# Seven block products for layer 1's up projection, and x kept in DRAM, in a two-layer trunk on one Trainium2 core

## The chip, the core and the metric

The kernel runs on one core of one Trainium2 chip. Its engines are TensorE (PE, with its weight loads as PEld), VectorE (DVE), ScalarE (ACT), GpSimd (POOL) and SyncE (SP), each with an instruction queue of its own that runs in order. The metric is the device time of one execution in microseconds (us). The frame in which the kernel is written (Tile) has a scheduler: the order of each engine's instructions follows from the program, its priorities and its tile pools, and is fixed before the run.

## What is computed

One step of a two-layer trunk on 640 tokens (512 sample tokens, 128 prompt tokens) with model width 1024. Layer 0 has a mixer of attention and gated MLP, layer 1 a bidirectional mLSTM; both end in the same FFN. The part that the change touches:

```python
def _modulate(x, w, shift, scale):
    return _rmsnorm(x, w) * (1 + scale) + shift

def _conv_ffn(h, w_up, cw, cb, w_down):
    a, g = jnp.split(h @ w_up, 2, axis=-1)
    return (jax.nn.gelu(_dwconv3(a, cw, cb)) * g) @ w_down

        h = _modulate(x, norm2_w[l], sh2, sc2)
        x = x + g2 * _conv_ffn(h, w_up[l], fconv_w[l], fconv_b[l], w_down[l])
    y_sample = _rmsnorm(x, final_norm_w)
```

`_dwconv3` is a three-point convolution along the tokens. All data are float32; the hidden width is 22 × 128.

## The kernel before

Activations lie with features on the 128 partitions and the 640 tokens along the free axis, as 8 tiles `x[k]` of 128 features (k-tiles) with two token halves of 320 (`HF`). A float32 product is made from three matmuls in the fp32r type: each operand is split in a high part (a cast, on ACT) and a low part (the difference, on DVE), and `proj` adds high·high, high·low and low·high. A product of 1024 features to 128 outputs for both halves is 8 × 3 × 2 = 48 matmuls of 320 columns.

Weights come through `wload`: one DMA on SP's queue into a tile `wraw`, the cast into `whi` (L181), the low part into `wlo` (L183), each in a ring of three tiles of 1024 columns in the pool `wp`, open for the whole kernel.

The FFN (`ffn`, for both layers the same code) runs over the 22 blocks f of the hidden width. Each block has two up products, a (s = 0) and g (s = 1). `conv3` copies a from PSUM to `fca` (L310, ACT), scales it (L313, ACT) and adds the two neighbours with four DVE instructions, for the 512 and the 128 tokens apart (L317, L319: 511 and 127 columns). Then come the gelu (L336, ACT), the product with g from PSUM (L337, DVE) and the split into high and low (L197 ACT, L198 DVE).

`GROUPS` cuts the 22 hidden tiles into three groups of 8, 7 and 7. After the first block of the following group come the 8 down products of the group before (`down`): each loads its weights, makes its product over the group's hidden tiles, and adds it into x[o] in SBUF with `residual` (L273: 320, 192 and 128 columns, as the token halves and the two segments cut them). The last group goes through `out_halves`: first the 8 outputs of token half 0, then the 8 of half 1, with sums of squares on ACT (L214) and POOL or DVE (L215); the steps of half 0's statistics and final norm (L224 to L240, L997) are run among half 1's products.

`start_three` starts the FFN: the first three up products, whose second token half is worked k-tile by k-tile as the norm of that half (`norm_k`: L247 DVE, L252 and L254 ACT, L256 DVE or POOL) delivers its tiles. In layer 1 `between` is empty.

The PSUM tiles come from `mm` (tags A with two buffers, B with one; each tile is two banks) and `misc` (two buffers of one bank).

Of the kernel before, what the change touches and what calls it, by code (L numbers as in the profile page):

```python
# [16 lines left out]
P = 128  # L17
# [9 lines left out]
GROUPS = ((0, 8), (8, 15), (15, 22))  # L27
# [18 lines left out]
def trunk(ctx: ExitStack, tc: tile.TileContext, I, O):  # L46
# [4 lines left out]
    wp = ctx.enter_context(tc.tile_pool(name="wp", bufs=3))  # L51
# [3 lines left out]
    misc = ctx.enter_context(tc.tile_pool(name="misc", bufs=2, space=PSUM))  # L55
    modx = ExitStack()
# [187 lines left out]
    def norm_k(pool, xk, rb, l, js, jc, k, hl, a0, a1):  # L244
# [3 lines left out]
        hf = pool.tile([P, w], F32, tag="hf", name=nm("hf"), bufs=2)  # L248
# [74 lines left out]
    def ffn(pool, x, hs, l, acc, between, done, late):  # L323
        def up(f, s):
            for _ in range(1 + (f %3 == 1)):
                if between:
                    between.pop(0)()
            hi, lo = wload(I["w_up"][l, f, s], KT * P)
# [13 lines left out]
        def down(g, hid):  # L342
            f0, f1 = GROUPS[g]
            for o in range(KT):
                if between:
# [776 lines left out]
```

## Time and profile before

| | |
|---|---|
| time, median of 3 runs (lowest to highest) | 1606.4 us (1603.39 to 1609.57) |
| the profiled execution's own time | 1606.81 us |
| its span, first to last instruction | 1605.0 us |
| mean granted clock of TensorE | 0.992 |
| layer 1's FFN in the chain | one piece of matmuls from 1146.90 us, 425.52 us long |

The page's first part gives the busy time of each engine as a share of the span. [...] The chain of waits follows the work that ended last back from step to step. A row of the table by line and form gives the busy time, the mean of one instruction in ns, and the idle time of the engine just ahead of these instructions with what ended it.

### The profile page before, as it was taken

Reading aid. Unit: us, or ns where it says so; the run is one execution under the profiler, and the core shown is the slowest. Engines: PE = TensorE matmul, PEld = TensorE weight load, DVE = VectorE, ACT = ScalarE, POOL = GpSimd, SP = SyncE. Lnnn points to the kernel's source line nnn. Section 1 sums busy time; section 2 is a strip of 40 time slices with the busy share of each in tenths; the row PEclk is TensorE's granted clock in tenths of the full one; section 3 lists DMA queues with packets and bytes.
Section 4 is the critical chain, followed back from the end, with each engine's and each line's share of the span. In section 5 each row is a group of like instructions: output and inputs, shape, how many; then the busy total and the mean of one; then the engine's idle time right before and its main releaser. Section 6 shows DMA issues by size and latency. Waiting matters only on the chain.

```text
span 1605.0 us, 26031 instructions
## 1 busy us (share of the span) xinstructions
PE 1561.2 (97%) x10560; PEld 1501.9 (94%) x10560; DVE 960.0 (60%) x1738; ACT 712.7 (44%) x1171; POOL 120.1 (7%) x116
## 2 busy tenths in 40 slices
PE   5999999999999999999989999999999999999997
PEld 4888889999999999999988999999999999999996
DVE  5547776769894889444775575667544334433445
ACT  5646665563312331334587564635633223312342
POOL 1100002300000000002300000013100000000012
PEclk9999999999999999999998999999999999999998
DMA  9424444436562555224523213234322222222233
GB/s 359 149 73 146 150 146 172 134 101 201 170 208 89 176 176 175 83 62 123 165 69 95 85 57 90 66 135 128 93 79 79 67 79 79 65 81 79 72 107 112
DMA packets 60167, 191.60 MB, mean 119 GB/s; under 512 B 6764, under 2 KB 10348, under 8 KB 59920
## 3 DMA queue, kind: packets, MB, share of 16 engines
q1 hardware_dynamic: 60048, 189.95, 37.2%
q8 instruction: 83, 1.36, 0.4%
q14 instruction: 36, 0.29, 0.1%
HBM read 181.95 MB, written 7.97 MB: 118 GB/s over the span
## 4 chain that ended last, share of the span: by engine, by line
PE 86%; DVE 6%; ACT 4%; issue 2%; DMA 2%; POOL 0%; SPq 0%; POOLq 0%; DVEq 0%; ACTq 0%
PE mm L193 72%; PE mm L827 2%; PE mm L805 2%; DVE wlo L183 1%; PE mm L401 1%; PE mm L403 1%; PE mm L802 1%; PE mm L402 1%; DMA mw<-w_mod 1%; PE misc L562 1%; ACT whi L181 1%; DVE xr L247 1%; ACT hf L252 1%; PE misc L109 1%; PE mm L532 1%
## 5 line engine op out<-in xcount | busy, mean ns | idle before, releaser
L193 PE MATMUL mm<-h,whi 128*128 128x320 f32 x3744 | 726.7, 312 | 3.4 <-ACT rows L612 1.6
L193 PEld LDWEIGHTS mm<-h,whi 128*128 128x128 f32 x3744 | 595.4, 189 | 9.7 <-ACT fca L310 1.9
L181 ACT CAST whi<-wraw 128x1024 fp32r<-128x1024 f32 (+2 forms) x229 | 233.0, 1019 | 586.6 <-PE mm L193 551.5
L193 PE MATMUL mm<-h,wlo 128*128 128x320 f32 x1872 | 444.8, 311 | 3.4 <-DVE wlo L183 3.4
L183 DVE TENSOR_TENSOR wlo<-wraw,whi 128x1024 fp32r<-128x1024 f32 (+2 forms) x229 | 272.7, 1191 | 232.8 <-ACT whi L181 226.3
L193 PE MATMUL mm<-hid,whi 128*128 128x320 f32 x1920 | 393.1, 310 | 1.8 <-ACT hid L197 0.7
L193 PEld LDWEIGHTS mm<-h,wlo 128*128 128x128 f32 x1872 | 318.9, 189 | 5.3 <-DVE wlo L183 4.2
L193 PEld LDWEIGHTS mm<-hid,whi 128*128 128x128 f32 x1920 | 310.4, 188 | 4.7 <-ACT hid L197 1.4
L193 PE MATMUL mm<-hid,wlo 128*128 128x320 f32 x960 | 255.5, 309 | 0.2 <-DVE wlo L183 0.2
L193 PEld LDWEIGHTS mm<-hid,wlo 128*128 128x128 f32 x960 | 169.7, 188 | 0.4 <-DVE wlo L183 0.4
L273 DVE SCALAR_TENSOR_TENSOR x<-mm,mod,x 128x192 f32<-128x192 f32 (+2 forms) x192 | 75.3, 433 | 139.9 <-PE mm L193 135.6
L136 DVE SCALAR_TENSOR_TENSOR mj<-mw,crow 128x1024 f32<-128x1024 f32 x112 | 136.6, 1219 | 1.0
L215 POOL TENSOR_TENSOR acc<-acc,sq 128x320 f32<-128x320 f32 x48 | 61.7, 1284 | 910.0 <-ACT sq L214 880.1
L337 DVE TENSOR_TENSOR fct<-fct,mm 128x640 f32<-128x640 f32 x44 | 36.1, 820 | 97.5 <-PE mm L193 94.1
L336 ACT ACTIVATE fct<-fct 128x640 f32<-128x640 f32 x44 | 32.3, 738 | 84.5 <-DVE fct L319 84.5
L252 ACT ACTIVATE hf<-xr,mod 128x192 f32<-128x192 f32 (+2 forms) x88 | 47.5, 575 | 22.6 <-DVE mod L174 8.8
L247 DVE TENSOR_TENSOR xr<-x,rb 128x320 f32<-128x320 f32 (+1 forms) x56 | 38.0, 694 | 24.9 <-ACT hf L252 13.7
L317 DVE SCALAR_TENSOR_TENSOR fct<-fca,vec,fct 128x511 f32<-128x511 f32 x88 | 44.9, 547 | 11.9 <-ACT fct L313 11.9
L319 DVE SCALAR_TENSOR_TENSOR fct<-fca,vec,fct 128x511 f32<-128x511 f32 x88 | 44.7, 544 | 0.0
L313 ACT ACTIVATE fct<-fca,vec 128x640 f32<-128x640 f32 x44 | 40.5, 925 | 1.3
L214 ACT ACTIVATE sq<-x 128x320 f32<-128x320 f32 x70 | 32.2, 468 | 16.7 <-DVE x L273 15.0
L541 ACT ACTIVATE p<-mm,mx 128x640 f32<-128x640 f32 (+1 forms) x40 | 28.4, 711 | 17.8 <-DVE mx L540 17.6
(249 smaller groups left out, 1491.6 us busy)
## 6 DMA issues: line engine op xcount, KB each, us to landing
wraw<-w_up SPq DMA_DIRECT2D x88, 512.0 KB, 3.7
mw<-w_modT SPq DMA_DIRECT2D x56, 512.0 KB, 4.3
wraw<-w_down SPq DMA_DIRECT2D x48, 448.0 KB, 3.3
mw<-w_mod SPq DMA_DIRECT2D x40, 512.0 KB, 5.9
wraw<-w_out SPq DMA_DIRECT2D x32, 512.0 KB, 3.6
wraw<-w_down SPq DMA_DIRECT2D x16, 512.0 KB, 3.6
x<-xT SPq DMA_DIRECT2D x16, 320.0 KB, 5.5
wraw<-w_qk SPq DMA_DIRECT2D x8, 512.0 KB, 3.5
```

The source lines that it names most:

```text
L136: V.scalar_tensor_tensor(out=junk, in0=w, scalar=1.0, in1=crow[:, r], op0=ALU.mult, op1=ALU.mult, accum_out=mod[:, l, j, k, r:r + 1])
L181: S.copy(hi[:, :n], raw[:, :n])
L183: V.tensor_tensor(out=lo[:, :n], in0=raw[:, :n], in1=hi[:, :n], op=ALU.subtract)
L193: T.matmul(ps[:, b, :HF], w, hs[k][:, part, b * HF:b * HF + HF], start=(k == 0 and i == 0), stop=(k == n - 1 and i == 2))
L215: (eng or V).tensor_tensor(out=acc[:, sl], in0=acc[:, sl], in1=sq, op=ALU.add)
L247: V.tensor_tensor(out=xr, in0=xk[:, a0:a1], in1=rb, op=ALU.mult)
L252: S.activation(out=hf[:, a:b], in_=xr[:, a:b], func=AF.Identity, scale=mod[:, l, jc, k, r:r + 1], bias=mod[:, l, js, k, r:r + 1])
L273: V.scalar_tensor_tensor(out=xo[:, a:b], in0=pa, scalar=mod[:, l, j, o, r:r + 1], in1=xo[:, a:b], op0=ALU.mult, op1=ALU.add)
L313: S.activation(out=t, in_=a, func=AF.Identity, scale=w1, bias=b)
L317: V.scalar_tensor_tensor(out=t[:, s + 1:e], in0=a[:, s:e - 1], scalar=w0, in1=t[:, s + 1:e], op0=ALU.mult, op1=ALU.add)
L319: V.scalar_tensor_tensor(out=t[:, s:e - 1], in0=a[:, s + 1:e], scalar=w2, in1=t[:, s:e - 1], op0=ALU.mult, op1=ALU.add)
L337: mark[0] = V.tensor_tensor(out=h2(t), in0=h2(t), in1=pg[:, :, :HF], op=ALU.mult)
```

## The change

Layer 0 keeps its code path. In layer 1's FFN:

- Blocks 0 to 2 (`PLAIN` = 3) are computed as before. Blocks 3 to 21 get their two up products for both token halves by a form of Strassen's scheme: the product is seen as 2 × 2 blocks (two halves of the 1024 features against a and g, two token halves) and formed by seven block products in place of eight. `prod` is one of them: 4 k-tiles × 3 = 12 matmuls of 320 columns. `fold_first` makes the first, `fold_main` five more, `fold_last` the last; it runs after the next block's `fold_first` in the program.
- The combinations of activations are made once: `fold_step`, four times, during blocks 1 and 2, on DVE, with a split on ACT and DVE. For that, `norm_k` keeps the norm's float32 result (f0, f1).
- The combinations of weights are made per block in `weights`: four DMAs of 256 KB, four adds on DVE, casts of 3 × 1024 and 512 on ACT, low parts of the same widths on DVE. Its rings are of their own (`zr`, `zw`, `rd`, `zd`); block 3 takes the old ring's tiles, which is then closed and opened again for the down weights with 640 columns.
- The partial results are gathered in two banks of one PSUM tile (b1, b4) and one of `misc` (b2), with ACT copies (L440, L441, L445, L447) and DVE adds (L449, L452, L455).
- The down products go in five groups of 5, 5, 4, 4 and 4 hidden tiles; two to four of them are issued per block. They no longer add into x in SBUF: `enter` stores x to DRAM (`xd2`), each down product loads its x[o] and stores it again on POOL's queue, and the memory of x serves the new rings. For the last group x is loaded back on SP's queue.

```diff
-GROUPS = ((0, 8), (8, 15), (15, 22))
+GROUPS = (((0, 8), (8, 15), (15, 22)), ((0, 5), (5, 10), (10, 14), (14, 18), (18, 22)))
+PLAIN = 3
...
-    wp = ctx.enter_context(tc.tile_pool(name="wp", bufs=3))
...
+    wx = ctx.enter_context(ExitStack())
+    ring = [wx.enter_context(tc.tile_pool(name="wp", bufs=3, side="right")), 1024]
...
     def wload(src, n, key="w"):
-        raw = wp.tile([P, 1024], F32, tag="wraw", name=nm("wraw"), bufs=3)
+        wp, width = ring
+        raw = wp.tile([P, width], F32, tag="wraw", name=nm("wraw"), bufs=3)
         nc.sync.dma_start(out=raw[:, :n], in_=src)
-        hi = wp.tile([P, 1024], F32R, tag="whi", name=nm("whi"), bufs=3)
+        hi = wp.tile([P, width], F32R, tag="whi", name=nm("whi"), bufs=3)
         S.copy(hi[:, :n], raw[:, :n])
-        lo = wp.tile([P, 1024], F32R, tag="wlo", name=nm("wlo"), bufs=3)
+        lo = wp.tile([P, width], F32R, tag="wlo", name=nm("wlo"), bufs=3)
         V.tensor_tensor(out=lo[:, :n], in0=raw[:, :n], in1=hi[:, :n], op=ALU.subtract)
-        return hi, lo
+        return hi, lo, raw
...
+        def down(g, hid, o, tag=None):
+            f0, f1 = groups[g]
+            if between:
+                between.pop(0)()
+            hi, lo, _ = wload(I[f"w_down{l}_{g}"][o], (f1 - f0) * P)
+            ps = mm_tile(tag)
+            if xd is not None:
+                xo = zq[0].tile([P, NT], F32, tag="xs", name=nm("xs"), bufs=3)
+                nc.gpsimd.dma_start(out=xo, in_=xd[o])
+            else:
+                xo = x[o]
+            proj(ps, hi, lo, hid)
+            residual(xo, ps, l, 5, o, 0, NT)
+            if xd is not None:
+                nc.gpsimd.dma_start(out=xd[o], in_=xo)
+
+        def prod(out, w, i, rhs, start):
+            for j in range(4):
+                c = slice(i * 512 + j * P, i * 512 + j * P + P)
+                for n, (h, part) in enumerate(((0, 0), (0, 1), (1, 0))):
+                    T.matmul(out, w[h][:, c], rhs(j, part), start=(start and j == 0 and n == 0),
+                             stop=(j == 3 and n == 2), skip_group_check=not start)
+
+        def split(w, src, n):
+            S.copy(w[0][:, :n], src[:, :n])
+            V.tensor_tensor(out=w[1][:, :n], in0=src[:, :n], in1=w[0][:, :n], op=ALU.subtract)
+            return w
+
+        def weights(f):
+            def pair(pool_, tag, n, bufs):
+                return [pool_.tile([P, n], F32R, tag=tag + p, name=nm(tag), bufs=bufs) for p in ("hi", "lo")]
+
+            def raw():
+                if f == PLAIN:
+                    return ring[0].tile([P, 1024], F32, tag="wraw", name=nm("wraw"), bufs=3)
+                return zp[0].tile([P, 1024], F32, tag="zr", name=nm("zr"), bufs=3)
+
+            def parts():
+                return pair(ring[0], "w", 1024, 3) if f == PLAIN else pair(zp[0], "zw", 1024, 5)
+
+            ra, rb, rc = raw(), raw(), raw()
+            if f == PLAIN:
+                rd, wd = zp[0].tile([P, 1024], F32, tag="zr", name=nm("zr"), bufs=3), pair(zp[0], "zw", 1024, 5)
+            else:
+                rd, wd = zq[0].tile([P, 512], F32, tag="rd", name=nm("rd"), bufs=1), pair(zq[0], "zd", 512, 1)
+            src = I["w_up"][l, f]
+            lo_, hi_ = slice(0, 512), slice(512, 1024)
+            nc.sync.dma_start(out=rd[:, lo_], in_=src[1][:, hi_])
+            nc.sync.dma_start(out=ra[:, lo_], in_=src[0][:, lo_])
+            nc.sync.dma_start(out=rc[:, hi_], in_=src[1][:, lo_])
+            nc.sync.dma_start(out=rb[:, lo_], in_=src[0][:, hi_])
+            V.tensor_tensor(out=ra[:, hi_], in0=rc[:, hi_], in1=rd[:, lo_], op=ALU.add)
+            wa = split(parts(), ra, 1024)
+            V.tensor_tensor(out=rb[:, hi_], in0=ra[:, hi_], in1=ra[:, lo_], op=ALU.add)
+            wb = split(parts(), rb, 1024)
+            V.tensor_tensor(out=rc[:, hi_], in0=rc[:, hi_], in1=ra[:, lo_], op=ALU.add)
+            V.tensor_tensor(out=rc[:, lo_], in0=rb[:, lo_], in1=rb[:, hi_], op=ALU.add)
+            wc = split(parts(), rc, 1024)
+            wd = split(wd, rd, 512)
+            return wa, wb, wc, wd
+        def fold_first(f, w):
+            px = mm_tile("A")
+            b1 = px[:, 0, :HF]
+            prod(b1, w[0], 0, lambda j, p: part_of(hs[j], p, 0), True)
+            return px
+
+        def fold_main(f, w, px):
+            b1, b4, b2 = px[:, 0, :HF], px[:, 1, :HF], aux[f % 2][:, :HF]
+            seed = f > PLAIN + 1
+            a = pool.tile([P, NT], F32, tag="fca", name=nm("fca"), bufs=1)
+            g = pool.tile([P, HF], F32, tag="fcg", name=nm("fcg"), bufs=2)
+            lo_, hi_ = slice(0, HF), slice(HF, NT)
+            prod(b4, w[0], 1, lambda j, p: fold[j](0, p), True)
+            with tc.high_priority(200):
+                S.copy(b2 if seed else a[:, lo_], b1)
+                S.copy(g, b4)
+            prod(b2, w[1], 0, lambda j, p: part_of(hs[j + 4], p, 0), not seed)
+            prod(b1, w[1], 1, lambda j, p: fold[j](1, p), False)
+            with tc.high_priority(200):
+                S.copy(a[:, hi_], b1)
+                if seed:
+                    S.copy(a[:, lo_], b2)
+                else:
+                    V.tensor_tensor(out=a[:, lo_], in0=b2, in1=a[:, lo_], op=ALU.add)
+            prod(b4, w[2], 0, lambda j, p: part_of(hs[j + 4], p, 1), False)
+            with tc.high_priority(200):
+                V.tensor_tensor(out=a[:, hi_], in0=b4, in1=a[:, hi_], op=ALU.add)
+            prod(b1, w[2], 1, lambda j, p: fold[j](2, p), False)
+            with tc.high_priority(200):
+                V.tensor_tensor(out=g, in0=b1, in1=g, op=ALU.add)
+            return conv(f, None, a), g
+
+        def fold_last(f, w, px, t, g):
+            b1 = px[:, 0, :HF]
+            prod(b1, w[3], 0, lambda j, p: fold[j](3, p), False)
+            for sl, q in ((slice(0, HF), b1), (slice(HF, NT), g)):
+                V.scalar_tensor_tensor(out=t[:, sl], in0=t[:, sl], scalar=-1.0, in1=q, op0=ALU.mult, op1=ALU.mult)
+            return store(f, t)
...
+        hids = [hidden(f) for f in range(PLAIN)]
+        enter()
+        zp[0] = zc.enter_context(tc.tile_pool(name="zp", bufs=1))
+        aux = [ms_tile() for _ in range(2)]
+        group_of = {f: g for g, (f0, f1) in enumerate(groups) for f in range(f0, f1)}
+        w = weights(PLAIN)
+        open_, todo = None, []
+        for f in range(PLAIN, NF):
+            g = group_of[f]
+            px = fold_first(f, w)
+            if open_ is not None:
+                hids.append(fold_last(*open_))
+            if f > PLAIN and group_of[f - 1] != g:
+                f0, f1 = groups[g - 1]
+                todo = [(g - 1, hids[f0:f1], o) for o in range(KT)]
+            if f == PLAIN:
+                t, gg = fold_main(f, w, px)
+                wx.close()
+                ring[:] = [wx.enter_context(tc.tile_pool(name="wq", bufs=3, side="right")), 640]
+                zq[0] = zc.enter_context(tc.tile_pool(name="zq", bufs=1))
+                nxt = weights(f + 1)
+                open_, w = (f, w, px, t, gg), nxt
+                continue
+            nxt = weights(f + 1) if f + 1 < NF else None
+            t, gg = fold_main(f, w, px)
+            n = min(len(todo), 4 if g and groups[g - 1][1] - groups[g - 1][0] == 5 else 3)
+            for i in range(n):
+                down(*todo.pop(0), "AB"[(n - i) % 2])
+            open_ = (f, w, px, t, gg)
+            w = nxt
+        hids.append(fold_last(*open_))
+        zc.close()
+        return hids[groups[-1][0]:]
...
+        def fold_step(j):
+            if j == 0:
+                tt.extend([hl_tile(hidp, "hid") for _ in range(2)])
+            d = hidp.tile([P, 4, HF], F32, tag="hid", name=nm("fd"), bufs=9)
+            b11, b12, b21, b22 = f0[j], f1[0][:, j], f0[j + 4], f1[1][:, j]
+            V.tensor_tensor(out=d[:, 0], in0=b11, in1=b12, op=ALU.subtract)
+            V.tensor_tensor(out=d[:, 2], in0=b22, in1=b12, op=ALU.subtract)
+            V.scalar_tensor_tensor(out=d[:, 1], in0=d[:, 0], scalar=-1.0, in1=b22, op0=ALU.mult, op1=ALU.subtract)
+            V.scalar_tensor_tensor(out=d[:, 3], in0=d[:, 1], scalar=-1.0, in1=b21, op0=ALU.mult, op1=ALU.subtract)
+            for i in range(2):
+                hilo(tt[2 * j + i], d[:, 2 * i:2 * i + 2].rearrange("p i c -> p (i c)"))
...
+        xd2 = dram.tile([KT, P, NT], F32, name="xd2")
+
+        def enter():
+            for k in range(KT):
+                nc.gpsimd.dma_start(out=xd2[k], in_=x[k])
+            sc.close()
+
+        hid = ffn(xp, x, hs, 1, [lambda j=j: fold_step(j) for j in range(4)], late, fold, enter, xd2)
+        ep = c0.enter_context(tc.tile_pool(name="ep", bufs=1))
+        acc = ep.tile([P, NT], F32, name=nm("acc"), tag="acc")
+        x = [ep.tile([P, NT], F32, name=nm("x"), tag=f"x{k}") for k in range(KT)]
...
+        for step in out_halves(ep, x, lambda o: I["w_down1_4"][o], 4, 1, 5, hid, acc, xd2, done1):
```

`part_of` in `proj` lets an operand be a function of part and half, `hidden` and `conv` are the former `hidden` in two pieces, and the host cuts `w_down` by the new groups.

What the scheduler makes of it on DVE, at the entry, where block 3's weights are first made. Before, this is the end of the convolution of block 1 and the beginning of that of block 2 (`wlo` are the low parts of up weights, `fct` the convolution, `hid` the hidden tile):

```order
L337 TENSOR_TENSOR fct_11662<-fct_11662,mm_11611 128x640 [waits PE_49,Activation_49]
L198 TENSOR_TENSOR hid_11602<-fct_11594,hid_11602 128x640 [waits Activation_49]
L183 TENSOR_TENSOR wlo_11800<-wraw_11796,whi_11798 128x1024 [waits DMAHW5_49]
L198 TENSOR_TENSOR hid_11670<-fct_11662,hid_11670 128x640 [waits Activation_49]
L183 TENSOR_TENSOR wlo_11855<-wraw_11851,whi_11853 128x1024 [waits DMAHW6_49,PE_49,Activation_49]
L317 SCALAR_TENSOR_TENSOR fct_11785<-fca_11783,vec,fct_11785 128x511 [waits Activation_49]
L317 SCALAR_TENSOR_TENSOR fct_11785<-fca_11783,vec,fct_11785 128x127
L319 SCALAR_TENSOR_TENSOR fct_11785<-fca_11783,vec,fct_11785 128x511 [waits DVE_49]
```

Now (`fd` are the folded activations and the tile written beside them their low part; `zr` and `wraw` block 3's raw weights, `w` their high and low parts):

```order
L204 TENSOR_TENSOR h_11368<-fd_11699,h_11368 128x640 [waits Activation_49]
L1177 SCALAR_TENSOR_TENSOR fd_11763<-fd_11763,f_1728_10727 128x320 [waits DVE_49]
L204 TENSOR_TENSOR hid_11611<-fd_11763,hid_11611 128x640 [waits Activation_49]
L326 SCALAR_TENSOR_TENSOR fct_11829<-fca_11827,vec,fct_11829 128x511
L204 TENSOR_TENSOR hid_11612<-fd_11763,hid_11612 128x640 [waits Activation_49]
L328 SCALAR_TENSOR_TENSOR fct_11829<-fca_11827,vec,fct_11829 128x511 [waits DVE_49]
L326 SCALAR_TENSOR_TENSOR fct_11829<-fca_11827,vec,fct_11829 128x127
L416 TENSOR_TENSOR wraw_11854<-wraw_11856,zr_11857 128x512 [waits DMASW4_49,DMASW5_49,DMASW3_49,DMASW6_49,DMASW2_49,DMASW7_49,DMASW1_49,DMAHW0_49,DMASW0_49,DMAHW6_49,PE_49,Pool_49]
L328 SCALAR_TENSOR_TENSOR fct_11829<-fca_11827,vec,fct_11829 128x127 [waits DVE_49]
L418 TENSOR_TENSOR wraw_11855<-wraw_11854 128x512 [waits DMAHW5_49,DVE_49]
L420 TENSOR_TENSOR wraw_11856<-wraw_11856,wraw_11854 128x512
L390 TENSOR_TENSOR w_11866<-wraw_11854,w_11865 128x1024 [waits Activation_49]
```

The first add of block 3's weights (L416) now stands behind the fold steps and most of block 2's convolution, and the first low part (L390) behind two more adds.

On PE, in the middle of the stage, where the b2 product of block 9 begins (`mm_13014` holds b1 and b4, `misc` b2, `mm_13329` a down product, `zw` the weights; `tt`, `h` and `hid` on L385 the activations):

```order
L385 MATMUL mm_13014<-h_11367,zw_12922 128x320 x2
L385 MATMUL mm_13014<-h_11367,zw_12923 128x320
L385 MATMUL mm_13014<-hid_11611,zw_12922 128x320 x2
L385 MATMUL mm_13014<-hid_11611,zw_12923 128x320
L199 MATMUL mm_13329<-hid_12908,wlo_13327 128x320
L385 MATMUL misc_11853<-h_11269,zw_12927 128x320 [waits Activation_49]
L385 MATMUL misc_11853<-h_11269,zw_12927 128x320
L385 MATMUL misc_11853<-h_11269,zw_12928 128x320
L385 MATMUL misc_11853<-h_11275,zw_12927 128x320 x2
L385 MATMUL misc_11853<-h_11275,zw_12928 128x320
L385 MATMUL misc_11853<-h_11317,zw_12927 128x320 x2
L385 MATMUL misc_11853<-h_11317,zw_12928 128x320
```

Before, products of 48 or 42 followed each other here with no wait for a copy within one; now one matmul of another product stands between the end of b4 and the product that waits for ACT's copy.

On SP's queue, at the change of rings after block 3:

```order
L414 DMA wraw_11856<-w_up 128x512 [waits DMAHW3_49,DVE_49]
L415 DMA wraw_11855<-w_up 128x512 [waits DMAHW4_49,DVE_49]
L412 DMA zr_11857<-w_up 128x512 [waits DMASW3_49,DMASW2_49,DMASW4_49,DMASW1_49,DMASW5_49,DMASW0_49,DMASW6_49,DVE_49,DMASW7_49,PE_49,Pool_49]
L413 DMA zr_11977<-w_up 128x512
L414 DMA zr_11979<-w_up 128x512
L415 DMA zr_11978<-w_up 128x512 [waits DMAHW0_49,DVE_49,Activation_49]
L412 DMA rd_11980<-w_up 128x512 [waits DMAHW6_49,DMAHW5_49,DMAHW7_49,DVE_49,PE_49]
L182 DMA wraw_12271<-w_down_0 128x640
L182 DMA wraw_12314<-w_down_0 128x640
L182 DMA wraw_12357<-w_down_0 128x640
```

Block 4's second g weight (`rd`) waits for PE, and the first loads of down weights stand behind it.

## Rows read from the trace of the kernel before

**Rows 1.** The page, part 1: busy us, share of the span, instructions of each engine.

```profile
PE 1561.2 (97%) x10560; PEld 1501.9 (94%) x10560; DVE 960.0 (60%) x1738; ACT 712.7 (44%) x1171; POOL 120.1 (7%) x116
```

**Rows 2.** Windows of 100 us: PE, PEld, DVE, ACT, POOL busy, PEclk, DMA share, GB/s.

```profile
400.00:500.00 100.00, 100.00 (x684) 100.00 (x683) 79.22 (x133) 25.15 (x28) 0.00 (x0) 1.00 0.57 178
...
1300.00:1400.00 100.00, 100.00 (x684) 100.00 (x683) 39.52 (x56) 32.52 (x38) 0.00 (x0) 1.00 0.24 73
```

**Rows 3.** Chain of waits, from 1130 us: start us, us, what.

```profile
1146.90 425.52 PE mm L193 x2898
```

**Rows 4.** DVE by line and form, 1100 to 1605 us: busy us, mean ns, idle before.

```profile
L183 DVE TENSOR_TENSOR wlo<-wraw,whi 128x1024 fp32r<-128x1024 f32 x56 | 68.8, 1228 | 95.5 <-ACT whi L181 95.5
...
L337 DVE TENSOR_TENSOR fct<-fct,mm 128x640 f32<-128x640 f32 x22 | 18.1, 821 | 56.7 <-PE mm L193 56.7
L317 DVE SCALAR_TENSOR_TENSOR fct<-fca,vec,fct 128x511 f32<-128x511 f32 x22 | 16.5, 751 | 7.6 <-ACT fct L313 7.6
...
L273 DVE SCALAR_TENSOR_TENSOR x<-mm,mod,x 128x320 f32<-128x320 f32 x24 | 13.2, 550 | 77.8 <-PE mm L193 77.8
L273 DVE SCALAR_TENSOR_TENSOR x<-mm,mod,x 128x192 f32<-128x192 f32 x30 | 12.3, 410 | 8.7 <-PE mm L193 8.6
...
L247 DVE TENSOR_TENSOR xr<-x,rb 128x320 f32<-128x320 f32 x16 | 10.3, 658 | 5.5 <-ACT rb L240 2.9 <-ACT hf L252 2.6
...
L317 DVE SCALAR_TENSOR_TENSOR fct<-fca,vec,fct 128x127 f32<-128x127 f32 x22 | 7.6, 345 | 0.0
...
L215 DVE TENSOR_TENSOR acc<-acc,sq 128x320 f32<-128x320 f32 x3 | 1.5, 485 | 0.7 <-ACT sq L214 0.7
```

**Rows 5.** DVE's operations in time, after 1144 us: start us, us, what.

```profile
1151.99 1.22 DVE L183 TENSOR_TENSOR wlo<-wraw,whi 128x1024 fp32r<-128x1024 f32 x1
1153.13 0.81 DVE L337 TENSOR_TENSOR fct<-fct,mm 128x640 f32<-128x640 f32 x1
1153.86 1.22 DVE L183 TENSOR_TENSOR wlo<-wraw,whi 128x1024 fp32r<-128x1024 f32 x1
```

**Rows 6.** ACT by line and form, 1100 to 1605 us.

```profile
L181 ACT CAST whi<-wraw 128x1024 fp32r<-128x1024 f32 x56 | 58.6, 1049 | 188.2 <-PE mm L193 183.3 <-issue 4.9
...
L313 ACT ACTIVATE fct<-fca,vec 128x640 f32<-128x640 f32 x22 | 20.3, 926 | 0.7
L336 ACT ACTIVATE fct<-fct 128x640 f32<-128x640 f32 x22 | 16.1, 738 | 41.3 <-DVE fct L319 41.3
...
L240 ACT COPY rb<-misc 128x320 f32<-128x320 f32 x2 | 0.8, 424 | 6.2 <-PE misc L236 6.2
```

**Rows 7.** PE after a wait: its timeline row, then windows as in rows 2.

```profile
789.38 0.83 PE L224 MATMUL misc<-ones,acc 128*128 128x1 f32 x6 [1.64 <-DVE acc L215]
...
791.00:792.00 1.00, 1.00 (x7) 1.00 (x6) 0.59 (x2) 0.00 (x0) 0.35 (x1) 0.62 0.85 283
792.00:793.00 1.00, 1.00 (x6) 1.00 (x5) 0.00 (x0) 0.00 (x0) 0.00 (x0) 0.50 0.45 180
...
794.00:795.00 1.00, 1.00 (x6) 1.00 (x6) 0.00 (x0) 0.00 (x0) 0.00 (x0) 0.68 0.00 0
795.00:797.00 2.00, 2.00 (x14) 1.84 (x13) 0.60 (x2) 0.44 (x2) 0.00 (x0) 1.00 0.00 0
```

**Rows 8.** Two more windows, columns as in rows 2.

```profile
1145.00:1150.00 5.00, 4.29 (x29) 3.96 (x28) 2.93 (x5) 4.79 (x7) 0.00 (x0) 1.00 0.29 70
...
870.00:890.00 20.00, 19.77 (x104) 17.17 (x104) 18.37 (x63) 12.98 (x36) 1.53 (x2) 1.00 0.38 99
```

**Rows 9.** DMA issues: KB each, median us from issue to landing.

```profile
xdr<-x SPq DMA_DIRECT2D x8, 320.0 KB, 2.2
...
x<-xdr SPq DMA_DIRECT2D x8, 320.0 KB, 5.5
...
ca<-state SPq DMA_DIRECT2D x8, 257.0 KB, 2.7
...
wraw<-w_hv SPq DMA_DIRECT2D x4, 256.0 KB, 3.4
```

More of the change, by code (lines that the diff above doesn't have):

```diff
@@ L321, in conv3, with ffn @@
         return a, t
-    def ffn(pool, x, hs, l, acc, between, done, late):
+    def ffn(pool, x, hs, l, between, late, fold=None, enter=None, xd=None):
+        abufs = 2 if fold is None else 1
+        groups = GROUPS[l]
+        zc = ExitStack()
+        zp, zq = [None], [None]
         def up(f, s):
-            for _ in range(1 + (f %3 == 1)):
+            for _ in range(1 + (f % 3 == 1)):
                 if between:
                     between.pop(0)()
-            hi, lo = wload(I["w_up"][l, f, s], KT * P)
+            hi, lo, _ = wload(I["w_up"][l, f, s], KT * P)
             ps = mm_tile()
@@ L339, in hidden, with store @@
+        def store(f, t):
+            hl = hl_tile(hidp, "hid") if fold is not None or f % 10 < 9 else hl_tile(pool, "hidx", 1)
             hilo(hl, t)
             return hl
[L342 to L345, printed above, removed]
-                    between.pop(0)()
-                hi, lo = wload(I[f"w_down{g}"][l, o], (f1 - f0) * P)
-                ps = mm_tile()
-                proj(ps, hi, lo, hid)
-                residual(x[o], ps, l, 5, o, 0, NT)
@@ L352, in ffn @@
-        first = start_three([I["w_up"][l, 0, 0], I["w_up"][l, 0, 1], I["w_up"][l, 1, 0]], hs, late)
-        pend = None
-        for g, (f0, f1) in enumerate(GROUPS):
-            hid = []
-            for f in range(f0, f1):
-                pa = first.pop(0) if first else up(f, 0)
-                pg = first.pop(0) if first else up(f, 1)
-                hid.append(hidden(f, pa, pg))
-                if pend is not None:
-                    down(*pend)
-                    pend = None
-            pend = (g, hid)
@@ new lines, in fold_last @@
+        def fold_last(f, w, px, t, g):
[3 more added lines that the diff above has]
+                V.scalar_tensor_tensor(out=t[:, sl], in0=t[:, sl], scalar=-1.0, in1=q, op0=ALU.mult, op1=ALU.mult)
+            return store(f, t)
+        first = start_three([I["w_up"][l, 0, 0], I["w_up"][l, 0, 1], I["w_up"][l, 1, 0]], hs, late)
+        first = list(first)
+        if fold is None:
+            pend = None
+            for g, (f0, f1) in enumerate(groups):
+                hid = []
+                for f in range(f0, f1):
+                    hid.append(hidden(f))
+                    if pend is not None:
+                        for o in range(KT):
+                            down(*pend, o)
+                        pend = None
+                pend = (g, hid)
+            return pend[1]
@@ new lines, in trunk @@
+        late = out_halves(sp, x, lambda o: I["w_out1"][o], KT, 1, 2, ys, acc, xdr, half)
+        tt += [hl_tile(hp, "h") for _ in range(2)]
+        btw = []
+        def fold_step(j):
[9 more added lines that the diff above has]
+                hilo(tt[2 * j + i], d[:, 2 * i:2 * i + 2].rearrange("p i c -> p (i c)"))
@@ L1078, in _layout @@
     dn = np.asarray(i["w_down"])
[L1079 to L1080 removed]
+    for l in range(2):
+        for g, (f0, f1) in enumerate(GROUPS[l]):
+            a[f"w_down{l}_{g}"] = wt(dn[l, f0 * P:f1 * P])
     t = np.arange(NS)
```

92 lines of the change are left out of this document (60 added, 32 removed).

## Prediction

> **What bounds the kernel now.** I read the busy times first, then the table of windows, then the chain of waits, then single operations. The span is filled by the tensor engine (PE): 1561.2 us, 97% [rows 1]. In the stretch that the change rewrites, layer 1's FFN, the windows show PE at 100.00 of 100 us with DVE at 39.5 and ACT at 32.5 [rows 2], and the chain is one piece of 425.52 us, 2898 matmuls and nothing else [rows 3]. One matmul of 320 columns thus costs 425.52/2898 = 146.8 ns, and there is no idle time to win: only fewer matmuls, or waits that did not exist, can move the end. The profiled execution took 1606.81 us; the median of the runs is 1606.4, so I sum against the first and shift by −0.4. No change is told from one by about 0.5% (8 us).
>
> **What is removed.** Each of the 19 blocks f = 3..21 has 84 matmuls of 320 columns in place of 96. Down products keep their count in total, only cut into other groups. So 19 × 12 = 228 matmuls go, and the order of PE's instructions has just that many fewer. 228 × 146.8 ns = **33.5 us saved**, if PE stays fed.
>
> **What is added, and what covers it.**
>
> *Per block f, on DVE:* four adds of 512, three low parts of 1024 and one of 512, two PSUM adds of 320, the convolution, two products of 320, one low part of 640. Prices are in [rows 4]: 1024 costs 1.23; 640 .82; the convolution two pairs of 511 and 127, 2 × (.75 + .345) = 2.18; 320 .485 as a plain add and .55 with a scalar. A 512 wide operation lies between 320 and 640: .69. Sum: 4 × .69 + 3 × 1.23 + .69 + 2 × .485 + 2.18 + 2 × .55 + .82 = 12.2 us. Back to back, starts lie closer than these durations (1.14 after a 1024 row, .73 after a 640 row [rows 5]); over 17 instructions at .08 each that is 10.8. PE's block is 84 × .1468 = 12.3. In a block without down products (9 of 19) DVE is thus nearly level with PE; in one with two to four, each product gives PE 24 or 30 matmuls (3.5 or 4.4 us) and DVE a low part of 640 at most and three residual pieces (.55, .41 and .345), about 2.1. On average it fits, with little slack. ACT has some 8 us per block (three casts of 1.05, four copies of .42, .93, .74 and less [rows 6]) and fits too.
>
> *Entry, f = 0..2 to f = 3.* In the order DVE now runs four fold steps between the convolutions: 8 adds (.485), 8 products with a scalar (.55), 8 low parts of 640 (.82), 14.8 us. The raw tile of block 3's first weight waits for the last reader of f0, and its first add (L416) stands behind all of them. From about 1151.9 us, where the first convolutions end before [rows 5], DVE has, up to the low part of block 3's first pair: 14.8 us of folds, one 1024 low part, two products and two low parts of 640, two convolutions, three adds of 512, one low part of 1024, 14.8 + 1.23 + 3.3 + 4.4 + 2.1 + 1.23 = 27.1, or 23.8 by spacing. It ends near 1175.7 to 1179. PE, released at 1146.9 [rows 3], has three products of 48, 21.1 us, and is done at 1168. Two matmuls (.3) need only the high part. **Loss 7.4 to 10.7; I take 7.5**, by the spacing, since rows without a wait lie that close. Before, DVE had only low parts and convolutions here, and waits of its own.
>
> *The clock after it.* [...] A pause of .71 us in 5 cost nothing (clock 1.00 in 1145 to 1150 [rows 8]).
>
> *Block 3 alone and the change of ring.* Block 3 is not overlapped with another: PE waits for a copy, two adds of .485 and their predecessors at three places; .65 + .73 + 1.4 = **2.8**. Block 4's rd tile lies where the old ring was, so its load is queued until PE has read block 3's last weights from that ring. Then come the load (2.7 to 3.4 us for 256 KB, as the state and w_hv rows [rows 9]; I take 3), an add .69, a cast 1.05 and a low part 1.23, less the 12 matmuls (1.76) that cover it and what of the adds was done before: 4.2; as the two first matmuls need no low part, I take **3.0**, bounds 1.5 and 4.5. A second fall of the clock, **1.6**, and .5 for block 4's own copies: **2.1**.
>
> *Blocks 5 to 20.* The order puts one other matmul between the b4 product and the b2 product, which waits for an ACT copy (.42) that itself waits for the end of b4: .42 + about .1 to .2 of hand-over less .15. The third product into b4 waits for ACT behind at most one cast of 1.05. Where down matmuls stand between, less remains. The trace of before has no such wait; bounds are 0 (all filled) and 1.2 per block (each behind a cast). I take .4, nearest to the copy's row. 16 × .4 = **6.5**.
>
> *Exit.* After block 21: add of g .49, product .55, cast .73, low part .82 with only four half products to fill. DVE's residuals of outputs 0 to 2 stand ahead of later low parts and wait for x, reloaded at 5.5 us for 320 KB [rows 9]: **3**, bounds 1 and 6. The last half: 8 products of 12 matmuls, 14.1 us, plus statistics; DVE has per output a low part of 512 (.69), a residual in two pieces of 192 and 128 (.41 and .345) and the first half's final scaling (about .55), 16 in all, and statistics on top: **1**, bounds 0 and 4.
>
> *The stream of x.* Each down product now loads and stores 320 KB on POOL's queue with three tiles. The nearest rows, on SP's queue, are 5.5 and 2.2 [rows 9]; with residual and wait some 9 us per tile, 3 us over three tiles, against 30 matmuls, 4.4 us. I cost it at nothing; cover: the matmuls of a burst. Extra traffic, 64 × 328 KB = 21 MB in some 360 us, 58 GB/s on top of 73, stays below the 178 GB/s at which PE stood at 100.00 [rows 2]. [...]
>
> **Sum.** Losses 7.5 + 1.6 + 2.8 + 3.0 + 2.1 + 6.5 + 3 + 1 = 27.5. 33.5 − 27.5 = 6.0 gained: 1606.8 − 6.0 = 1600.8 for the profiled execution, **1600.4 us** for the median. Taking the bounds that are likeliest to move together, its own range is 1592 to 1609.
>
> **Rivals.**
> (A) *The stalls are filled.* Back-to-back spacing holds, the scheduler's fillers close the copies, the reload overlaps. Entry and swap then cost 9 instead of 17, blocks 5 to 20 2, exit and tail 3 of 4: losses some 14, time 1606.4 − 19 = 1588. For it: DVE's spacing [rows 5]; against: 24 us of DVE work in 21 us of PE work at the entry is in the order itself.
> (B) *DVE and ACT become the bound* in the fold blocks, ending slower. Each block needs three short hand-overs on strict queues full of 1.05 and 1.23 us operations; if the copy or add that PE waits for lands behind one of them, 17 to 19 blocks × about 1.2 = 20 to 23 in place of 6.5, plus DVE longer where POOL is at work: L247 took .658 on average [rows 4], where its plain form is .485. Losses 27.5 + 14 + 3 to 4 = 45; time 1606.4 + 11.6 = 1618. It decides from (33.5 − 21) / 16 = .8 us of idle per block upwards. For: the block's DVE sum, 10.8 to 12.2 of 12.3. Against: the order gives those copies places ahead of casts.
> (C) *The clock falls once per block.* A fall costs 1.6 us [rows 7]; 17 of them are 27, time 1627. Against it: in 870 to 890 us PE lost .23 of 20 us and had weight loads in only 17.17, at clock 1.00 [rows 8]. [...]
> (D) *The x stream runs late*, a load queued behind the store before it. From about 13 us for load, residual and store together (three products) it shows; at 1.5 us in each of the 10 blocks with products, 15 us on top of the forecast, time 1615.
> That the matmuls are not removed is excluded: the order has 228 fewer.
>
> **Chances.** Forecast .50, A .22, B .18, C .04, D .06. Of the forecast's .50, .17 lies under 1598.4 and .02 over 1614.4. Faster by over 0.5%: .22 + .17 = .39. Slower: B .16, C .04, D .04 and .02 = .26. Same: .35. The likeliest own range is 1592 to 1609; the range that leaves out no more than 2 in 10 takes in most of A, B and D, 1585 to 1620: outside lie the better end of A (.06), the worse end of B (.06), C and the end of D.
>
> **What would show it.** Right: PE with 228 matmuls fewer; one hole of about 7 us some 20 us after the FFN starts, ended by DVE's low part, and a second of 3 to 5 some 15 us later; clock .50 behind both; windows of the fold blocks at PE 95 to 98 of 100, DVE 80 to 90 in them, no window of .50 clock. Wrong: PE below 93 of 100 in the fold blocks with idle ended by ACT copies (B); PEclk below 1.00 in every block (C); idle ended by POOL's queue (D); no hole at the entry (A). Most of the doubt is in the .4 us per block, which stands 16 times in the sum and has no row of its own.

## The result and the profile after

The changed kernel takes 1617.86 us (median of 5 runs, 1616.21 to 1622.37) against 1607.16 us (1603.39 to 1609.57) of the kernel before in the same comparison: ratio 1.0072, 95% interval 1.0049 to 1.0094. It is slower by 0.7%, where 1600.4 us had been forecast. The value lies inside the range of 1585 to 1620 and, as a time, at rival B.

The matmuls did go: the page's first part counts 10332 where there were 10560 [rows 1], and PE's busy time fell by 15.6 us. The span grew by 11.1 us. DVE has 130 us more to do.

```profile
span 1616.1 us, 26343 instructions
PE 1545.6 (96%) x10332; PEld 1472.6 (91%) x10332; DVE 1090.2 (67%) x1999; ACT 761.2 (47%) x1288; POOL 158.4 (10%) x188
```

Where the time went is read best by cutting layer 1's FFN at PE's waits: the three plain blocks, block 3 with the change of rings, the folded blocks that follow, the exit, the last half. Windows of the changed kernel, columns as in rows 2 (PEclk is the clock that TensorE was granted, as a share of its full one):

```profile
1150.50:1178.40 27.90, 21.47 (x144) 21.14 (x144) 25.68 (x46) 16.82 (x23) 0.00 (x0) 0.93 0.17 58
1178.40:1206.56 28.16, 21.99 (x120) 20.02 (x120) 18.22 (x27) 13.15 (x19) 1.68 (x3) 0.89 0.36 119
1206.56:1554.00 347.44, 338.06 (x2248) 329.86 (x2249) 245.10 (x415) 144.21 (x214) 32.38 (x60) 1.00 0.44 134
1554.00:1577.00 23.00, 21.51 (x136) 19.74 (x136) 10.71 (x21) 8.15 (x16) 1.33 (x2) 1.00 0.45 147
1577.00:1617.00 40.00, 26.75 (x168) 24.73 (x166) 27.00 (x57) 11.93 (x24) 12.59 (x14) 0.85 0.43 136
```

What a stretch lost is its length less its matmuls at 146.8 ns (from [rows 3]):

| stretch | worked out | lost, us | forecast, us |
|---|---|---|---|
| output projection, between its two statistics | 30.1 against 27.5 before | 2.7 | 0 |
| entry | 27.9 − 144 × .1468 | 6.8 | 7.5 |
| block 3, rings, clock | 28.2 − 120 × .1468 | 10.5 | 1.6 + 2.8 + 3.0 + 2.1 = 9.5 |
| folded blocks | 347.4 − 2248 × .1468 | **17.4** | 6.5 |
| exit | 23.0 − 136 × .1468 | 3.0 | 3 |
| last half from 1577, over the same of before | (39.1 − 168 × .1468 = 14.4) − (28.0 − 111 × .1468 = 11.7), to the last instruction | 2.7 | 1 |

Together 43.1 us, with 33.5 us saved and a start 1.2 us later in this execution, which the change doesn't touch. The span's growth of 11.1 asks for 44.6 − 1.2 = 43.4, so the table leaves out 0.3 us.

The folded blocks are the surprise. The table by line and form shows what DVE waited for between 1206 and 1550 us: its first add of each block's weights (L416) sits idle 32.9 us, all of it for the load of one tile.

```profile
L416 DVE TENSOR_TENSOR zr<-zr,rd 128x512 f32<-128x512 f32 x17 | 11.7, 691 | 32.9 <-DMA rd<-w_up 32.9
```

The chain of waits has this piece ten times. Once it reads (start us, us, what):

```profile
1246.48 0.70 DVE zd L390
1247.20 4.08 DMA rd<-w_up
1251.30 0.70 DVE zr L416
1252.05 0.94 issue
1252.99 1.03 ACT zw L389
1254.40 2.02 PE mm L385 x12
```

And ACT's operations in time show why PE waits at its end:

```profile
1252.03 1.99 ACT L389 CAST zw<-zr 128x1024 fp32r<-128x1024 f32 x2 [1.34 <-DVE zr L416]
1253.93 0.42 ACT L445 COPY fca<-mm 128x320 f32<-128x320 f32 x1
```

`rd` has one buffer (`bufs=1`). Its next load can start only when DVE has taken the low part of the last one (L390), which itself waits for PE to have read the block before out of `zd`, also a single buffer. SP's waits between 1206 and 1550 us show it for 15 of the 16 loads (waiting line, releaser, us in total, times, longest):

```profile
SPq L412 <- DVE zd L390: 42.2, 15, 4.6
```

The load takes 2.6 to 4.3 us (median 3.6); only then come the add, two casts, and behind these two casts, in ACT's queue, the copy L445 of the running block (in the rows above it starts 1.95 us after PE's last matmul of the product that it reads, at the end of the casts), for which PE's next product into the same PSUM tile waits (it writes b4, the tile's other bank; L445 reads b1). So a late load of the **next** block's weights holds up the copy of **this** one.

### The profile page after: what moved, and what is told of

Read it like the earlier page. It is cut to its first block, busy times and chain, and to the rows that moved or that the text cites. A ratio compares the mean times of both kernels' runs of the same rounds, so it can differ in the third digit from the quotient of the medians.

```text
span 1616.1 us, 26343 instructions
## 1 busy us (share of the span) xinstructions
PE 1545.6 (96%) x10332; PEld 1472.6 (91%) x10332; DVE 1090.2 (67%) x1999; ACT 761.2 (47%) x1288; POOL 158.4 (10%) x188
## 4 chain that ended last, share of the span: by engine, by line
PE 79%; DVE 9%; ACT 5%; DMA 4%; issue 2%; POOL 0%; SPq 0%; DVEq 0%; POOLq 0%; ACTq 0%
PE mm L199 54%; PE mm L385 10%; DMA rd<-w_up 2%; PE mm L974 2%; PE mm L952 2%; DMA mw<-w_mod 1%; PE mm L548 1%; DVE wlo L186 1%; PE mm L550 1%; PE mm L549 1%; PE misc L709 1%; PE mm L949 1%; ACT whi L184 1%; PE misc L385 1%; DVE xr L253 1%
## 5 line engine op out<-in xcount | busy, mean ns | idle before, releaser
L199 PE MATMUL mm<-h,whi 128*128 128x320 f32 x2480 | 490.7, 313 | 3.3 <-ACT rows L759 1.6
L199 PEld LDWEIGHTS mm<-h,whi 128*128 128x128 f32 x2480 | 396.7, 190 | 9.3 <-ACT fca L319 1.9
L184 ACT CAST whi<-wraw 128x1024 fp32r<-128x1024 f32 (+3 forms) x207 | 193.7, 938 | 424.1 <-PE mm L199 387.6
L186 DVE TENSOR_TENSOR wlo<-wraw,whi 128x1024 fp32r<-128x1024 f32 (+3 forms) x207 | 228.4, 1105 | 131.0 <-ACT whi L184 130.0
L199 PE MATMUL mm<-h,wlo 128*128 128x320 f32 x1240 | 299.3, 312 | 2.6 <-DVE wlo L186 2.6
L199 PEld LDWEIGHTS mm<-h,wlo 128*128 128x128 f32 x1240 | 212.6, 190 | 4.3 <-DVE wlo L186 3.1
L385 PE MATMUL mm<-h,zw 128*128 128x320 f32 x597 | 104.7, 312 | 11.6 <-ACT fca L445 6.0
L385 PEld LDWEIGHTS mm<-h,zw 128*128 128x128 f32 x597 | 90.6, 188 | 16.0 <-ACT fca L445 8.4
L390 DVE TENSOR_TENSOR zw<-zr,zw 128x1024 fp32r<-128x1024 f32 (+1 forms) x55 | 65.5, 1210 | 4.4 <-ACT zw L389 4.3
L385 PE MATMUL mm<-tt,zw 128*128 128x320 f32 x330 | 59.4, 313 | 1.8 <-DVE fcg L455 1.0
L281 DVE SCALAR_TENSOR_TENSOR xs<-mm,mod,xs 128x320 f32<-128x320 f32 (+2 forms) x96 | 36.6, 433 | 33.8 <-PE mm L199 33.8
L385 PEld LDWEIGHTS mm<-tt,zw 128*128 128x128 f32 x330 | 50.4, 188 | 4.1 <-DVE fca L452 1.8
L253 DVE TENSOR_TENSOR xr<-x,rb 128x320 f32<-128x320 f32 (+1 forms) x56 | 37.4, 683 | 24.5 <-ACT hf L259 11.1
```

The source lines that it names most:

```text
L199: T.matmul(ps[:, b, :HF], w, part_of(hs[k], part, b), start=(k == 0 and i == 0), stop=(k == n - 1 and i == 2))
L253: V.tensor_tensor(out=xr, in0=xk[:, a0:a1], in1=rb, op=ALU.mult)
L281: V.scalar_tensor_tensor(out=xo[:, a:b], in0=pa, scalar=mod[:, l, j, o, r:r + 1], in1=xo[:, a:b], op0=ALU.mult, op1=ALU.add)
L385: T.matmul(out, w[h][:, c], rhs(j, part), start=(start and j == 0 and n == 0), stop=(j == 3 and n == 2), skip_group_check=not start)
L390: V.tensor_tensor(out=w[1][:, :n], in0=src[:, :n], in1=w[0][:, :n], op=ALU.subtract)
```

## The experiments

All ratios are to the kernel before, run on the same chip; the two groups of kernels (first four, then three) each have their own runs of it. The changed kernel stood 10.7 us over its own (1617.86 − 1607.16); what an edit gives back is told against that. In single traces I compare from the first statistics matmul of the output projection to the end, since the start of that stretch differs by some 5 us between executions, for no edit made here. The stretch is 1605.0 − 1099.3 = 505.7 us before and 1616.1 − 1100.5 = 515.6 after.

**Two buffers for rd.**

```diff
-                rd, wd = zq[0].tile([P, 512], F32, tag="rd", name=nm("rd"), bufs=1), pair(zq[0], "zd", 512, 1)
+                rd, wd = zq[0].tile([P, 512], F32, tag="rd", name=nm("rd"), bufs=2), pair(zq[0], "zd", 512, 1)
```

> Edit: the tile rd (block f+1's second half of g's weights) gets two buffers in place of one; nothing else. Theory A (the load of rd is in the chain of every block: it can start only when block f's rd has been split, and the next block's first add, cast and low part wait for it): DVE's 32.9 us of idle time ahead of the first add (L416) falls below 10, PE's waits for the copy L445 and the casts L389 between 1206 and 1560 us fall from 9.3 to under 3, that stage loses some 7 instead of 16.7 us, time 1606 to 1612. Rival B (the copies that PE waits for stand behind 1.05 us casts whatever rd does; DVE and ACT queues are the limit): the idle time before L416 goes, but PE waits as long for other rows, time 1616 to 1619.

Measured: 1606.72 us, ratio 1.0008 (0.9992 to 1.0023), 1.0 us over before where the changed kernel stood 10.7 over: 9.7 given back. The stretch from the first statistics to the end is 506.1, 9.5 less. The same 2248 matmuls of the folded blocks now take 337.9 instead of 347.4 us, the whole of it:

```profile
1203.40:1541.30 337.90, 336.19 (x2248) 329.86 (x2249) 245.39 (x415) 144.63 (x215) 32.31 (x60) 1.00 0.44 137
```

PE's longest waits between 1206 and 1550 us, first in the changed kernel, then with two buffers (columns as for SP's waits):

```profile
PE mm L385 <- ACT fca L445: 6.0, 5, 1.4
PE mm L385 <- ACT zw L389: 2.9, 3, 1.3
```

```profile
PE mm L385 <- ACT fca L445: 1.3, 1, 1.3
PE mm L385 <- DVE fca L452: 0.4, 1, 0.4
```

Two shorter waits of the changed kernel, .7 and .4 us, aren't shown. The second list starts a little later in the program, as this execution runs some 3 us ahead: over the same 2248 matmuls it also has block 4's copy L441, 1.2 us, so 2.9 us of waits in all against 10.0. Theory A holds in its size and its rows; DVE's idle time ahead of L416 was a little over what was expected (11.3 us, 8.6 of it still for rd). Rival B falls: DVE and ACT do as much work as in the changed kernel in this stretch (245 and 145 us) and PE hardly waits. The loss that is left, 337.9 − 330.0 = 7.9 us, is near the 6.5 of the forecast. Most of it shows at PE's weight loads (1203.4 to 1541.3 us):

```profile
PEld mm L385 <- DVE fca L452: 2.7, 12, 0.6
PEld mm L385 <- ACT fca L445: 2.5, 6, 1.5
PEld mm L385 <- ACT fcg L441: 1.5, 1, 1.5
```

The edit changes more than the buffer, as the scheduler orders the queues anew for it. In ACT's, for one, the two casts that stood next to each other ahead of L445 are parted, and one of them now stands ahead of L440. That one buffer is the cause of the 9.5 us is shown; how much of them is the earlier load's and how much the new order's, no run here tells apart. Nor does one tell what two PSUM tiles for b1 and b4, in place of one, would spare.

**x's stores on SP's queue.**

```diff
-                nc.gpsimd.dma_start(out=xd2[k], in_=x[k])
+                nc.sync.dma_start(out=xd2[k], in_=x[k])
```

> Edit: the eight stores of x at the start of the FFN are issued on SP's queue instead of POOL's; DVE's order is the same. Theory A (the stores on POOL's queue push POOL's sums of squares and low parts against DVE's, a 1024 low part takes 2.94 instead of 1.23 us, PE idles 1.9 us at 1118 and its clock falls): the FFN's first released matmul comes at about 1147 instead of 1150.5 us, time 1613 to 1616. Rival B (DVE's order, with the norm's steps ahead of the low parts, does it): the stretch before 1150 us is unchanged, time 1617 to 1619.

Measured: 1611.96 us, ratio 1.0039 (1.0022 to 1.0056), 6.2 over before, so 4.5 given back by the medians. The trace gives the edit less: first statistics to the end 513.7, 1.9 under the changed kernel. Of the 2.5 us won at the place itself about 1 went again at the change of rings, where the clock fell in this execution (.83 over 1190 to 1200 us; ten matmuls took 2.70 us, 1.73 in the changed kernel). Which of the two is nearer stays open. The place is as expected: between the two statistics 27.6 us instead of 30.1. In the changed kernel PE's row at that place and DVE's and POOL's operations in time are

```profile
1118.71 0.42 PE L199 MATMUL mm<-hid,wlo 128*128 128x320 f32 x1 [1.91 <-DVE wlo L186]
```

```profile
1115.71 2.94 DVE L186 TENSOR_TENSOR wlo<-wraw,whi 128x1024 fp32r<-128x1024 f32 x1
```

```profile
1115.28 0.56 POOL L1186 DMA_DIRECT2D xd<-x  x1 [1.23 <-DVE x L281]
1115.86 0.89 POOL L264 TENSOR_TENSOR h<-f,h 128x320 fp32r<-128x320 f32 x1
1116.70 0.86 POOL L221 TENSOR_TENSOR acc<-acc,sq 128x320 f32<-128x320 f32 x1
1117.52 1.86 POOL L264 TENSOR_TENSOR h<-f,h 128x320 fp32r<-128x320 f32 x1
```

POOL waits at the store's issue for x, and then runs its two additions straight against DVE's low part, which takes 2.94 instead of 1.23 us. With the stores on SP it takes 1.88, PE idles 1.51 instead of 1.91 us, and the clock stays at 1.00 (in the changed kernel it is .50 from 1120 to 1123 us):

```profile
1112.33 1.88 DVE L186 TENSOR_TENSOR wlo<-wraw,whi 128x1024 fp32r<-128x1024 f32 x1
1114.27 0.42 PE L199 MATMUL mm<-hid,wlo 128*128 128x320 f32 x1 [1.51 <-DVE wlo L186]
```

**The same stores, added to the kernel before.**

```diff
         late = out_halves(xp, x, lambda o: I["w_out1"][o], KT, 1, 2, ys, acc, xdr,
                    lambda b: norm_half(xp, x, acc, 1, 3, 4, hs, b))
+        xd2 = dram.tile([KT, P, NT], F32, name="xd2")
+        for k in range(KT):
+            nc.gpsimd.dma_start(out=xd2[k], in_=x[k])
```

> The kernel before, with eight stores of x to DRAM on POOL's queue added at the start of layer 1's FFN (they are not read). Theory A of the stores: FFN start 2 to 4 us later than before, time 1609 to 1611. Rival B (DVE's order in the changed kernel): no change, 1606 to 1608.

Measured: 1605.93 us, ratio 0.9999 (0.9985 to 1.0012); 27.4 us between the statistics, as before. Theory A as written falls: the stores alone cost nothing. With the second experiment it takes both: the stores on POOL and the changed kernel's DVE order, in which a low part stands just where POOL is let go. This is inferred from the two runs; a third, with the new order and no stores at all, wasn't made.

**One more plain block.**

```diff
-PLAIN = 3
+PLAIN = 4
```

> Edit: PLAIN = 4, so one more block of the old kind stands between the fold steps and the first folded block; 12 matmuls more. Theory A (27 us of DVE work against 21 us of PE work at the entry makes the hole): with 14.1 us more of PE work the hole of 7.0 us and the 3 us at half clock behind it go, price 1.8: time 1608 to 1611. Rival B (the first folded block's weights only come later too, because their loads wait for the old ring): hole of 4 to 7 us at the entry stays, time 1617 to 1620.

Measured: 1611.92 us, ratio 1.0031 (1.0013 to 1.0048), 6.2 over before: 4.5 given back, 3.9 by the trace. That is less than theory A had expected, for reasons that the rows show. The hole at the entry, in the changed kernel and here:

```profile
1178.41 0.90 PE L385 MATMUL mm<-h,w 128*128 128x320 f32 x2 [6.41 <-ACT w L389]
1179.93 3.03 PE L385 MATMUL mm<-h,w 128*128 128x320 f32 x10 [0.62 <-DVE w L390]
```

```profile
1186.12 0.56 PE L385 MATMUL mm<-h,w 128*128 128x320 f32 x2 [1.68 <-ACT w L389]
1187.38 1.74 PE L385 MATMUL mm<-h,w 128*128 128x320 f32 x10 [0.70 <-DVE w L390]
```

The hole shrinks to 2.4 us and the clock holds there (1.00 over 1180 to 1190 us; 10 matmuls in 1.74 instead of 3.03 us). It falls later instead, at the change of rings, where ten matmuls take 2.48 us (1.73 in the changed kernel; .84 over 1200 to 1210 us). Theory A holds in its mechanism; 2.4 us of the hole stay. Rival B's hole of 4 to 7 us isn't there.

**The edits together.** Two buffers for rd and the stores on SP:

> Two buffers for rd and x's stores on SP's queue. If the rd chain (11 us) and the late start of the FFN (2.7 us from the first to the second statistics of the output projection: 30.1 against 27.5 us before) are separate losses, they add: 2 to 3 us under the kernel with rd alone, 1603 to 1605, so 2 to 3 us faster than before. If both shorten the same wait, 1606 to 1607.

Measured: 1603.96 us, ratio 0.9994 (0.9983 to 1.0006); first statistics to the end 504.4, 1.7 under two buffers alone. Against its own runs of before that is −.5, so 11.2 given back, as the trace has it (515.6 − 504.4). By the traces the two add (9.5 + 1.9 = 11.4); by the medians of the single edits (9.7 + 4.5 = 14.2) they don't in full. The 2 to 3 us under the kernel before that were expected didn't come: the interval takes in no difference.

With PLAIN = 4 on top:

> The same and PLAIN = 4. If the entry's hole is a loss of its own, as it was without the other edits (hole 2.4 instead of 7.0 us, no fall of the clock, 1.8 us more matmuls): 4 to 6 us under the one before, 1598 to 1600, ratio to before about 0.996. If the time saved at the entry comes back at the change of rings: 1602 to 1605.

Measured: 1599.96 us, ratio **0.9965 (0.9952 to 0.9977)**: faster than the kernel before by 0.35%, and than the changed kernel by 1.1%. The entry is its own loss: 4.0 us by the medians, the low end of what was expected, and 5.8 by the traces (504.4 − 498.6). Part of what the entry gives comes back at the change of rings, where the clock falls as in the run with PLAIN = 4 alone (.94 over the 27.7 us from 1183.4): ten matmuls take 3.04 us instead of 1.73. First the changed kernel, then this one:

```profile
1200.57 1.73 PE L385 MATMUL mm<-h,zw 128*128 128x320 f32 x10 [0.72 <-DVE zw L390]
```

```profile
1203.15 3.04 PE L385 MATMUL mm<-h,zw 128*128 128x320 f32 x10 [0.76 <-DVE zw L390]
```

The folded blocks lose 326.9 − 2185 × .1468 = 6.1 us:

```profile
1211.10:1538.00 326.90, 326.65 (x2185) 320.44 (x2186) 236.27 (x401) 137.58 (x204) 32.98 (x61) 1.00 0.45 140
```

With PLAIN = 5. Under this value the program never issues the eight down products of the first group; the kernel leaves them out, 240 matmuls or 35.2 us of PE.

> The same with PLAIN = 5: another 12 matmuls, 1.8 us. If PLAIN = 4 has left a hole of some 2 us at the entry, that goes too and the time is level with PLAIN = 4 (within 1 us), 1598 to 1600. If the entry was limited by the loads into the old ring, the hole of 2 us stays: 1600 to 1602.

Measured: 1566.45 us; with the 35.2 us that are left out 1601.7, 1.7 over PLAIN = 4. At the entry PE still waits 1.55 and .85 us:

```profile
1198.41 0.56 PE L385 MATMUL mm<-h,w 128*128 128x320 f32 x2 [1.55 <-ACT w L389]
1199.83 2.04 PE L385 MATMUL mm<-h,w 128*128 128x320 f32 x10 [0.85 <-DVE w L390]
```

So the last 2.4 us at the entry aren't DVE's fold steps. Nor are they the old ring's, as the second expectation had it: the loads into that ring were issued from 1166.4 to 1178.2 us. The late load is that of the first folded block's second g weight, whose tile `zr` lies in the new pool:

```profile
SPq L412 <- PE mm L199: 14.8, 1, 14.8
1193.42 0.33 SPq L412 DMA_DIRECT2D zr<-w_up  x1
```

This pool takes the memory of x and of what lay beside it, `hb` among it, a part of the norm's result. PE's last matmul that reads `hb` starts at 1193.03, 24 matmuls before the end of the last plain block, and the load starts as it ends. With PLAIN = 4 alone the two stand alike, at 1180.62 and 1181.00 us. In the changed kernel this load waits for the last fold step instead. A further plain block doesn't take this wait away and costs its 12 matmuls. As the kernel leaves work out, its total is a weak witness; the rows are the evidence.

## Why the prediction was wrong

**What held.** 228 matmuls went. The entry's hole is where and as long as forecast (6.4 + .6 us against 7.5), ended by the cast and the low part of block 3's first pair. Block 3 with the change of rings and the clock lost 10.5 against 9.5, and its parts come near too. The entry's second wait, for the low part, lies in this window (1.2 us; the entry is then 8.0 in all against 7.5). The clock after it cost 2.3 us instead of 1.6, an estimate (the four windows of before from 791 to 795 us, at .62, .50, .50 and .68, lose 1.7 [rows 7]): from 1179.93 to the b2 product 22 matmuls took 5.50 us, which are 3.23 at 146.8 ns.

```profile
1185.43 1.92 PE L385 MATMUL misc<-h,w 128*128 128x320 f32 x12
```

The copies and adds of block 3 cost 2.9 (2.8 forecast), the change of rings 3.1 (3.0). Behind it block 4's copies cost 1.0 (.5), and the clock, for whose second fall 1.6 stood in the sum, didn't fall in the two traces of the changed kernel and of two buffers alone (ten matmuls in 1.73 us in both); it did in the four others that have three or four plain blocks (2.32 to 3.04 us). The exit lost its 3. Rival A falls with the hole at the entry. The stream of x cost nothing, as reckoned: DVE's residuals into xs waited 33.8 us for PE and never for a load, so rival D falls, with 3.8 us for load and store each.

**What failed.** The step "Blocks 5 to 20": 16 × .4 = 6.5, for "an ACT copy (.42) that itself waits for the end of b4", found 17.4. The .1 to .2 us of hand-over in it was an estimate; at 1247.69 us the trace has .04 from the end of b4 to the copy's start and .05 from the copy's end to the b2 product. The size of the hand-overs themselves was about right, as the kernel with two buffers shows (7.9) and the fastest complete one (6.1), but partly by luck: the copy that the step named, ahead of the b2 product (L440), isn't among the waits of the kernel with two buffers, where the add L452 and the copy L445 are. What the step lacked is the load of `rd`. At the change of rings I counted just this chain (a load that can't start, then add, cast and low part), for block 4 only; the other blocks' loads have no term in the sum. But `rd` and `zd` have one buffer each, so the chain closes in every block: end of PE's reading, split, load, add, cast. The order of SP's queue had shown the wait for the first of them, and DVE's own sum per block (10.8 to 12.2 of 12.3 us) held only work and no such wait. A second buffer for that one tile gave back 9.5 us in this stage and 9.7 in the time; that alone turns the 0.7% loss into no difference.

The second error is a term of nought: the stretch ahead of the FFN, 2.7 us. The change was costed from the FFN's start on, but the eight stores of x are issued in the projection before it, on POOL's queue between POOL's sums. The prediction asked what POOL's queue does to the stream of x in the blocks, not what these first stores do to POOL's sums.

**Rival B** had the time, 1618, and half of its sign (waits ended by ACT copies, but not PE below 93 of 100), and not the cause: that its time came true is luck. It said that DVE and ACT are full. The windows show DVE at 245 of 347 us, 71%, well under the 80 to 90 that I had named for the stage, with 32.9 us of idle time for one load. The copy did land behind two casts, and these were late by the load. PE's share was 97.3 of 100, in the band that stood for the forecast being right: of the 17.4 us 8.0 lie inside PE's busy time, which is 150.4 ns for a matmul instead of 146.8, so the share didn't show the loss. **Rival C** falls: the clock was 1.00 through all 347 us, in spite of the many short waits.

## What to carry over

For each tile of a pipeline, write down the loop from one load to the next: who must be done with the buffer, how long the load takes, who waits for it. Here, in most blocks, this loop left less slack than the load takes (DVE stood idle for it up to 3.35 us), and a single small buffer cost more than the whole hand-over between engines (9.5 us against 7.9); it was 2 KB per partition. And a copy that the running step needs inherits the lateness of work of the next step that stands ahead of it on the same in-order queue (L445 above, 1.95 us); no run here put the copy first.

## What the runs showed of the hardware

- At the same place in the output projection the clock stayed at 1.00 after an idle time of PE of 1.51 us and fell to .50 after 1.91 us. At the entry, after 6.41 us, PE ran some 6.4 us at .50, .62 of them waiting. The length of the idle time doesn't tell by itself: ahead of block 4 the clock stayed at 1.00 after waits of 1.88 and .72 us in the changed kernel, while with two buffers and the stores on SP, after waits of 1.50 and .73 us, ten matmuls took 2.32 us where the changed kernel's took 1.73.
- A low part of 1024 on DVE took 2.94 us when two POOL additions ran into it, 1.7 longer than the usual 1.23; the two took .89 and .86 us, 1.75 together. The third POOL addition then took 1.86 us instead of .88. DVE's row starts .15 us ahead of the first POOL addition and yet is the one that grew; no run here shows the cause.
- 320 KB on POOL's queue took 3.8 us from issue to landing for the loads and for the stores of the stream, and 2.8 us for the first eight stores.
